# Attention over every 64th key on one core: scores with queries on partitions, the maximum subtracted ahead of exp, weights normalised and turned over by TensorE

## The chip, the cores and the metric

The kernel runs on one core of a Trainium2 chip. The core has five instruction streams that meet only at semaphores: TensorE (PE: matrix products, its weight loads shown as PEld), VectorE (DVE), ScalarE (ACT), GpSimd (POOL) and SyncE (SP, which here only issues DMAs). Sixteen DMA engines carry them out. The metric is the device time of one execution in microseconds (us).

## What is computed

Q, K and V have 8 batches, 12 heads, 1024 rows and 64 columns, in float32. Each of the 1024 queries of a head attends to the 16 keys at rows 0, 64, 128 and so on:

```python
attend_positions = np.arange(0, seq, stride)            # stride 64: 16 keys
scores = np.einsum('bhqd,bhkd->bhqk', q, k) * scale     # scale = 1/8
weights = np.exp(scores - np.max(scores, axis=-1, keepdims=True))
weights = weights / (np.sum(weights, axis=-1, keepdims=True) + 1e-10)
result[:, :, i, :] = np.einsum('bhqk,bhkd->bhqd', weights, v)[:, :, 0, :]
```

Q is read whole (25.17 MB) and the output is written whole (25.17 MB). Of K and V only 1,536 rows of 256 bytes each are read.

## The kernel before

The 96 heads are taken in 24 groups of four (`NG`, `HG`). A group's Q is 1 MB: `load` brings it into one of ten buffers `qn`, 8 KB on each of 128 partitions, and a group's output leaves from one of eight buffers `out_sb` by `store`, 1 MB at a time, or 2 MB for the pairs near the end. In DRAM each partition's piece of an output is written as runs of 4 KB (`send`).

What one group needs, in order:

- `cast`: Q to bfloat16, half by ACT (L328) and half by POOL (L330), into one of two `qb`. POOL's half waits for ACT's, and stands for both.
- `transpose`: DVE turns 32 by 32 blocks of bfloat16 pairs over (L335), so that pairs of the 64 columns lie on partitions, 32 for each of the four heads.
- `score_products`: four products of 512 columns (L469). The stationary operand is `k_t`, the keys of the four heads laid out in blocks with zeros between; Q is the moving one. The result `sc` has **keys on partitions**: 128 partitions are 4 heads by 2 halves of the queries by 16 keys, the free axis holds 512 queries.
- exp by ACT in two instructions of 64 partitions (L353), straight from PSUM, without a maximum, into `w_all`, where zeros stand between.
- `outputs`: eight products of 260 columns (L497), in blocks of 3, 2 and 3 (`blocks`). The stationary operand is a block of `w_all`. The moving one is `v_all`: the values of the group, masked so that each head has its own 64 columns, and four columns of ones, which give the sum of each head's weights. POOL makes it with `values` (L318).
- the division, behind the product: DVE takes reciprocals of the four sums (L453) and multiplies (L459) for blocks 0 and 1. Block 2 is copied by ACT (L383) and multiplied by POOL (L385).

`Program` holds one list of operations, in the order in which the code writes them, with what each reads and writes. `plan` works out the semaphore waits from it, and each engine gets its own operations in that order; nothing is reordered on the chip. PE and DVE run loops written by hand, `pe_stream` with 4 groups in a turn and `dve_stream` with 8. ACT, POOL and SP are unrolled. In the main loop, while group g's output is made, group g+2 is transposed, group g+3 is cast and the scores of g+1 are made.

SP's stream has ten loads first, then `load(g+10)` and `store(g)` in turns, each waiting for what it needs: a load for the buffer to be read out, a store for the output of its group. The very last store is issued behind the loop and waited for at the end.

Of the kernel before, what the change touches and what calls it, by code (L numbers as in the profile page):

```python
# [10 lines left out]
FP32 = mybir.dt.float32  # L11
# [31 lines left out]
class Program:  # L43
# [7 lines left out]
    ENGINES = ("PE", "DVE", "ACT", "POOL", "SP")  # L51

    def __init__(self, nc, tc):
        self.nc, self.tc, self.ops = nc, tc, []
        self.writer, self.readers = {}, {}

    def op(self, engine, fn, reads=(), writes=(), after=(), lane=None, gate=None, gates=(), looped=False, last=False):
# [12 lines left out]
        for k in writes:  # L70
            self.writer[k], self.readers[k] = i, []
        self.ops.append(dict(
            engine=engine, fn=fn, lane=lane or engine, deps=deps, own=own,
            gate=gate, gates=gates, last=last, looped=looped or engine == "PE",
# [3 lines left out]
    def plan(self):  # L78
# [12 lines left out]
        for i, o in enumerate(self.ops):  # L91
            e, waits, gate_waits = o["engine"], [], list(o["gates"])
            for gate, n in o["gates"]:
                assert carriers[gate][n - 1] < i, (i, gate, n)
                learn(e, carriers[gate][n - 1])
            for d in sorted(o["deps"], reverse=True):
# [5 lines left out]
                assert not o["looped"], ("needs more gates", i, e, d, p["lane"])  # L102
# [3 lines left out]
                if d is None:  # L106
                    d = self.ops.index(p)
# [14 lines left out]
        for i, o in enumerate(self.ops):  # L122
            transfer = o["lane"] != o["engine"]
            o["step"] = 16 if transfer else int(i in signals or o["engine"] == "PE" or o["last"])
# [3 lines left out]
            assert o["step"] or o["gate"] or not o["looped"], (i, o)  # L128
# [5 lines left out]
    def emit(self, loops):  # L134
# [7 lines left out]
        gates = {name: nc.alloc_semaphore(f"gate_{name}") for name in names}  # L142
        with self.tc.tile_critical(no_gpsimd_drain=True):  # L143
            for e in ("ACT", "DVE", "POOL"):
                engines[e].addr_align(128, max_nops=0)
            for o in self.ops:
                if o["looped"]:
                    continue
                for gate, n in o["gates"]:
                    engines[o["engine"]].wait_ge(gates[gate], n)  # L150
                for d in o["waits"]:
                    p = self.ops[d]
                    engines[o["engine"]].wait_ge(sems[p["lane"]], p["count"])
                r = o["fn"]()
                if o["gate"]:
                    r.then_inc(gates[o["gate"]], 1)
                elif o["step"]:
                    r.then_inc(sems[o["lane"]], o["step"])
            nc.sync.wait_ge(sems["POOL"], counts["POOL"])
            for loop in loops:  # L160
                loop(sems, gates)
# [5 lines left out]
def kernel(  # L167
# [8 lines left out]
    nc = tc.nc  # L176
# [10 lines left out]
    KW = P + NK  # L187
    TURN = 4
    ROUNDS = 8
    assert B * H == NG * HG and S == 1024 and D == 64 and NK == 16 and NG % TURN == NG % ROUNDS == 0  # L190
    QBUFS = 10
    OBUFS = 8

# [10 lines left out]
    out_all = [sb.tile([P, 2, 4, 8, D], FP32, name=f"out_sb{i}") for i in range(OBUFS // 2)]  # L204
    out_sb = [out_all[i // 2][:, i % 2] for i in range(OBUFS)]
    qt = [sb.tile([P, 32 * D], BF16, name=f"qt{i}") for i in range(2)]
    rec = [sb.tile([P, 8, 4], FP32, name=f"rec{i}") for i in range(2)]
    w_all = sb.tile([P, 2, 8, P], BF16, name="w_all")
    v_all = sb.tile([P, 4, 4 * D + 4], BF16, name="v_all")
    w_bufs, v_bufs = [w_all[:, i] for i in range(2)], [v_all[:, i] for i in range(4)]  # L210
    k_t = sb.tile([P, NG + 1, 2, KW], BF16, name="k_t")
# [3 lines left out]
    perm_v = sb.tile([P, 2, 2, 2, 2, NK], BF16, name="perm_v")  # L215
# [127 lines left out]
    def scores(g):  # L343
# [4 lines left out]
        if g == NG:  # L348
            return
# [197 lines left out]
```

## Time and profile before

| | us |
|---|---|
| median of 3 runs | 127.6 (127.23 to 128.01) |
| the profiled execution's own time | 127.66 |
| its span, from first to last instruction | 125.9 |
| busy: DVE, ACT, POOL, PE | 90.7, 80.9, 78.2, 66.5 |
| DMA packets' share of 16 engines' span | 96.9% |

A row of the groups reads: line, engine, operation, what is written and read with its shape (partitions by elements), how often; then busy time in all and mean ns of one; then the idle time of the engine ahead of it and who ended that. A row of the timeline begins with start and length in us, and an [idle] at its end is what the engine waited ahead of it. In a row of windows stand, behind the stretch and its length, the busy time of PE, PEld, DVE, ACT and POOL, then the granted TensorE clock (1 is full speed), the mean busy share of the DMA engines and their GB/s. The shapes show the free elements of one partition; a matmul's `128x512` has 512 columns.

### The profile page before, as it was taken

The numbers are of one execution on the slowest core, as the hardware profiler recorded it, in microseconds if no ns is written. First come the engines' busy times: TensorE is split into PE (matmuls) and PEld (weight loads), VectorE is DVE, ScalarE is ACT, GpSimd is POOL, SyncE is SP. The second block draws the span as 40 slices with busy tenths as digits, with TensorE's granted clock in tenths as the row PEclk, the third lists the DMA queues.
The fourth block names the chain that finished last, engine by engine and source line by source line (L and its number), as shares of the span: only waits on it lengthen the run. The fifth ranks groups of instructions, "written<-read, shape, count | busy, mean of one in ns | idle before, by whom it ended". The sixth has DMA issues, their size and how long they took to land.

```text
span 125.9 us, 1283 instructions
## 1 busy us (share of the span) xinstructions
PE 66.5 (53%) x296; PEld 29.7 (24%) x296; DVE 90.7 (72%) x161; ACT 80.9 (64%) x103; POOL 78.2 (62%) x89
## 2 busy tenths in 40 slices
PE   0005472887777796466555666478664663840000
PEld 0001130343333333233212333233332320410000
DVE  2996457978669669989997999966999794970000
ACT  4270943686966786989999799968698655711000
POOL 4074247387865956988999699986699851534000
PEclk9999999755685559999999999955999999755555
DMA  1999989899899999899798998999998999999991
GB/s 43 423 312 479 479 354 500 354 479 448 344 417 458 403 435 495 359 474 469 338 515 354 411 515 341 430 458 398 440 482 364 450 427 422 422 422 422 424 424 70
DMA packets 7140, 51.15 MB, mean 406 GB/s; under 512 B 3808, under 2 KB 3808, under 8 KB 3808
## 3 DMA queue, kind: packets, MB, share of 16 engines
q1 hardware_dynamic: 7136, 51.12, 96.9%
q14 instruction: 4, 0.03, 0.1%
HBM read 25.95 MB, written 25.17 MB: 406 GB/s over the span
## 4 chain that ended last, share of the span: by engine, by line
DMA 25%; PE 20%; DVE 20%; ACT 13%; POOL 8%; issue 4%; SPq 1%; ACTq 0%; DVEq 0%; POOLq 0%
DMA out_dram<-out_sb 18%; DVE out_sb L459 12%; PE o L497 10%; PE sc L469 10%; DMA qn<-in_Q_dram 7%; ACT w_all L353 5%; ACT out_sb L383 4%; DVE qt L335 4%; POOL out_sb L385 4%; ACT qb L328 3%; DVE rec L453 3%; POOL qb L330 2%; DVE v_rep L312 1%; POOL v_all L318 1%; SPq L236 1%
## 5 line engine op out<-in xcount | busy, mean ns | idle before, releaser
L497 PE MATMUL o<-v_all,w_all 128*128 128x260 bf16 x192 | 38.8, 327 | 28.5 <-DVE out_sb L459 24.2
L385 POOL TENSOR_TENSOR out_sb<-out_sb,rec 128x768 f32<-128x768 f32 x24 | 35.3, 1472 | 25.3 <-ACT out_sb L383 25.3
L469 PE MATMUL sc<-qt,k_t 128*128 128x512 bf16 x100 | 33.3, 464 | 16.5 <-DVE qt L335 12.3
L459 DVE TENSOR_TENSOR out_sb<-o,rec 128x768 f32<-128x768 f32 (+1 forms) x48 | 39.6, 825 | 1.6
L353 ACT ACTIVATE w_all<-sc 64x512 bf16<-64x512 f32 x48 | 35.2, 733 | 7.3 <-DMA out_dram<-out_sb 3.5
L335 DVE STREAM_TRANSPOSE qt<-qb 128x1024 int32<-128x1024 int32 x26 | 31.6, 1214 | 3.6 <-POOL qb L330 3.5
L497 PEld LDWEIGHTS o<-v_all,w_all 128*128 128x128 bf16 x192 | 18.3, 112 | 52.4 <-DVE out_sb L459 33.0
L383 ACT COPY out_sb<-o 128x768 f32<-128x768 f32 x24 | 19.2, 799 | 16.5 <-DVE rec L453 16.2
L328 ACT CAST qb<-qn 128x1024 bf16<-128x1024 f32 x24 | 25.0, 1045 | 4.3 <-DVE v_rep L312 1.4
L330 POOL CAST qb<-qn 128x1024 bf16<-128x1024 f32 x24 | 24.9, 1039 | 1.9 <-DMA qn<-in_Q_dram 1.7
L453 DVE RECIPROCAL rec<-o 128x12 f32<-128x12 f32 (+1 forms) x72 | 15.4, 213 | 11.7 <-PE o L497 10.9
L318 POOL TENSOR_TENSOR v_all<-mask,v_rep 128x256 bf16<-128x256 bf16 x24 | 16.0, 670 | 4.2 <-DVE v_rep L312 4.1
L469 PEld LDWEIGHTS sc<-qt,k_t 128*128 (+1 forms) x100 | 10.9, 110 | 27.7 <-issue 11.7
L257 DVE MEMSET k_t<- 128x3600 uint32 x1 | 3.1, 3058 | 2.3 <-issue 2.3
L312 DVE CAST v_rep<-o 128x768 bf16<-128x768 f32 x2 | 1.9, 939 | 2.6 <-PE o L302 2.6
L291 DVE COPY k_t<-k_r 32x256 bf16<-32x256 bf16 x8 | 3.2, 395 | 0.1
L277 ACT CAST k_bf<-k_raw 128x256 bf16<-128x256 f32 (+1 forms) x2 | 0.9, 508 | 2.6 <-DMA k_raw<-in_K_dram 2.6
L266 POOL COPY v_all<-s_sel 128x16 bf16<-128x16 bf16 x1 | 0.2, 197 | 3.7 <-DVE s_sel L262 3.7
L277 ACT ACT_TABLE_LOAD x1 | 1.3, 1283 | 1.3 <-SPq L143 1.3
L302 PE MATMUL o<-v_bf,perm_v 128*128 128x384 bf16 x4 | 1.5, 520 | 1.0 <-POOL v_bf L416 1.0
L291 ACT COPY k_t<-k_r 32x128 bf16<-32x128 bf16 x4 | 1.2, 295 | 0.8 <-DVE k_r L279 0.7
L291 POOL COPY k_t<-k_r 32x128 bf16<-32x128 bf16 x4 | 1.2, 290 | 0.3
(13 smaller groups left out, 5.1 us busy)
## 6 DMA issues: line engine op xcount, KB each, us to landing
qn<-in_Q_dram SPq DMA_DIRECT2D x24, 1024.0 KB, 15.4
out_dram<-out_sb SPq DMA_DIRECT2D x16, 1024.0 KB, 14.0
out_dram<-out_sb SPq DMA_DIRECT2D x4, 2048.0 KB, 17.4
k_raw<-in_K_dram SPq DMA_DIRECT2D x1, 384.0 KB, 4.2
v_raw<-in_V_dram SPq DMA_DIRECT2D x1, 384.0 KB, 6.7
```

Source lines behind the costliest of these rows:

```text
L291: op(e, lambda: fn(k_t[dst : dst + 32, 2 * part.start + c : 2 * part.stop : 2, :, col : col + NK], k_r[src : src + 32, part].rearrange("p ...
L318: op("POOL", lambda: nc.gpsimd.tensor_tensor(out=v[:, 0 : 4 * D].rearrange("p (s d) -> p s d", s=4), in0=mask, in1=v_rep[:, g // 2, g % 2] ...
L328: op("ACT", lambda: nc.scalar.copy(b[:, half:], q[:, half:]), reads=[f"qn{g % QBUFS}1"], writes=[f"qb{g % 2}1"])
L330: op("POOL", lambda: nc.gpsimd.tensor_copy(out=b[:, 0:half], in_=q[:, 0:half]), reads=[f"qn{g % QBUFS}0"] + [f"qb{g % 2}1"] * (g >= 2) + [ ...
L335: return nc.vector.transpose(qt[g % 2].bitcast(I32), qb[g % 2].bitcast(I32))
L353: op("ACT", lambda a=a, wa=wa: nc.scalar.activation(out=_ap_with(wa, [wa.ap[0], [P, 8], [1, 2], [2, 32]], extra_offset=64 * a), in_=sc[64 ...
L383: op("ACT", lambda: nc.scalar.copy(to, o), reads=[o_key], writes=[to_key, f"copy{g}"], after=[sums])
L385: op("POOL", lambda: nc.gpsimd.tensor_tensor(out=to, in0=to, in1=by, op=ALU.mult), reads=[to_key, r_key], writes=[to_key], last=g == NG - 1)
L453: sums = dve.reciprocal(r, o_ps[(3 * j + c) % 2][:, 0 : blocks[c][1], 4 * D : 4 * D + 4])
L459: dve.tensor_tensor(out=to, in0=o, in1=by, op=ALU.mult).then_inc(gates["scaled"], 1)
L469: r = pe.matmul(sc_ps[g % 2], lhsT=k_t[:, k, f, NK * (1 - e) : NK * (1 - e) + P], rhs=_ap_with(qt[g % 2], [qt[g % 2].ap[0], [D, 8], [16 * ...
L497: r = pe.matmul(o_ps[(3 * j + c) % 2][:, i, 0 : 4 * D + 4], lhsT=w_bufs[j % 2][:, i0 + i], rhs=v_bufs[j % 4], start=True, stop=True,)
```

## The change

The softmax is moved from the output side to the score side. For each group:

- `cast` also reorders rows, and is split 3/8 ACT (768 elements) and 5/8 POOL (1280). `transpose` writes with a step of four.
- `scores`: Q is now the stationary operand (every second column of `qt`) and the keys the moving one: 16 products of 64 columns, which give 128 queries on partitions and, for 8 tiles of queries by 4 heads, 16 keys along the free axis.
- `lowered`: DVE takes the maximum over each 16 keys (512 elements to 32) and subtracts it (512), from PSUM into `low`, in float32.
- `raised`: one exp of 128 by 512 on ACT, from SBUF.
- `sums`: DVE adds up each 16 (512 elements to 32) and takes 32 reciprocals.
- `weights`: POOL multiplies the 512 weights by their reciprocals into bfloat16.
- `across`: PE turns the weights over with four products against the identity, 128 columns each; `weight_rows`: DVE copies the result (512) from PSUM.
- `outputs`: eight products of 256 columns with 64 rows of weights each; `evict`: ACT copies them out in two instructions of 1024 elements. No division is left there; the columns of ones, the zeros of `w_all` and their memset go.
- `send` writes runs of 2 KB.

In iteration i of the main loop each engine has, in this order:

| engine | operations |
|---|---|
| DVE | `weight_rows(i)`, `transpose(i+3)`, `sums(i+1)`, `lowered(i+2)` |
| PE | `scores(i+2)`, `outputs(i)`, `across(i+1)` |
| ACT | `cast(i+4)`, `evict(i)` twice, `raised(i+2)` |
| POOL | `cast(i+4)`, `values(i+1)`, `weights(i+1)` |

The loops of PE and DVE have two groups in a turn (`PERIOD`), and the last four iterations are unrolled. SP has 15 loads ahead of the first store, then stores and loads in turns.

```diff
-    TURN = 4
-    ROUNDS = 8
+    HK = HG * NK
+    NT = 8
+    PERIOD = 2
+    AHEAD = 4
...
-    o_ps = [ps.tile([P, 3, 512], FP32, name=f"o{i}") for i in range(2)]
+    wt_ps = [ps.tile([P, 512], FP32, name=f"wt_ps{i}") for i in range(2)]
+    o_ps = ps.tile([P, 4, 512], FP32, name="o")
...
+    cut = 5
     def cast(g):
-        q, b = qn[g % QBUFS], qb[g % 2]
-        op("ACT", lambda: nc.scalar.copy(b[:, half:], q[:, half:]),
+        q = qn[g % QBUFS].rearrange("p (j t d) -> p t j d", j=4, t=NT)
+        b = qb[g % 2].rearrange("p (t j d) -> p t j d", t=NT, j=4)
+        op("ACT", lambda: nc.scalar.copy(b[:, cut:], q[:, cut:]),
            reads=[f"qn{g % QBUFS}1"], writes=[f"qb{g % 2}1"])
-        op("POOL", lambda: nc.gpsimd.tensor_copy(out=b[:, 0:half], in_=q[:, 0:half]),
+        did["cast", g] = op("POOL", lambda: nc.gpsimd.tensor_copy(out=b[:, :cut], in_=q[:, :cut]),
            reads=[f"qn{g % QBUFS}0"] + [f"qb{g % 2}1"] * (g >= 2) + ["turn"] * (g < 2),
...
+    def scores(g, i=None):
+            for x in range(NT):
+                t = x // 4 * 4 + x % 2 * 2 + x // 2 % 2
+                for f in range(2):
+                    r = nc.tensor.matmul(
+                        sc_ps[g % 2][:, HK * x : HK * x + HK],
+                        lhsT=q[:, 4 * D * t + f : 4 * D * (t + 1) : 2],
+                        rhs=k_t[:, k, f], start=f == 0, stop=f == 1,
+                    )
...
+    def lowered(g, i=None):
+        maxima = op("DVE", lambda: nc.vector.tensor_reduce(
+            out=top, in_=sc, op=ALU.max, axis=mybir.AxisListType.X,
+        ), reads=[f"sc{g % 2}"], writes=["top"], gates=[did["scored", g]], gate="own", turn=i)
+        op("DVE", lambda: nc.vector.tensor_tensor(
+            out=low[g % 2], in0=sc, in1=top.unsqueeze(2).to_broadcast([P, NT * HG, NK]),
+            op=ALU.subtract,
...
+    def raised(g):
+        did["raised", g] = op("ACT", lambda: nc.scalar.activation(
+            out=ex[g % 2], in_=low[g % 2], func=AF.Exp, bias=0.0, scale=scale,
...
+    def sums(g, i=None):
+        added = op("DVE", lambda: nc.vector.tensor_reduce(
+            out=total, in_=ex[g % 2], op=ALU.add, axis=mybir.AxisListType.X,
+        ), reads=[f"ex{g % 2}"], writes=["total"], gates=[did["raised", g]], gate="own", turn=i)
+        op("DVE", lambda: nc.vector.reciprocal(rec[g % 2], total),
...
+    def weights(g):
+        did["weighed", g] = op("POOL", lambda: nc.gpsimd.tensor_tensor(
+            out=wn[g % 2], in0=ex[g % 2],
+            in1=rec[g % 2].unsqueeze(2).to_broadcast([P, NT * HG, NK]), op=ALU.mult,
...
+    def across(g, i=None):
+            for b in range(NT // 2):
+                r = nc.tensor.matmul(
+                    wt_ps[g % 2][:, P * b : P * b + P], lhsT=w[:, P * b : P * b + P],
+                    rhs=identity, start=True, stop=True,
+                )
...
+    def weight_rows(g, i=None):
+        did["evened", g] = op("DVE", lambda: nc.vector.tensor_copy(
+            out=wt[g % 2], in_=wt_ps[g % 2].rearrange("p (b q) -> p b q", b=NT // 2),
...
+    def outputs(g, i=None):
+                for x in range(4 * n, 4 * n + 4):
+                    b, side = x // 2, x % 2
+                    rows = slice(HK * side, HK * side + HK)
+                    r = nc.tensor.matmul(
+                        o_ps[:, 2 * n + side, HG * D * (b % 2) : HG * D * (b % 2 + 1)],
+                        lhsT=wt[g % 2][rows, b],
+                        rhs=vm[g % 2][rows].rearrange("p h d -> p (h d)"),
...
+            gates = [did["evened", g], did["sent", g - 1]]
...
+    def evict(g):
+        for n in range(2):
+            i = op("ACT", lambda n=n: nc.scalar.copy(
+                out_sb[g % OBUFS][:, :, 4 * n : 4 * n + 4].rearrange("p h t d -> p t h d"),
+                o_ps[:, 2 * n : 2 * n + 2].rearrange("p b (t h d) -> p (b t) h d", t=2, h=HG),
...
     def send(g, n):
-            _ap_with(out, [[16 * D, P], [2 * SD, 2 * n], [1, 16 * D]], g * HG * SD),
+            _ap_with(out, [[NT * D, P], [SD, HG * n], [1, NT * D]], g * HG * SD),
...
+    for i in range(-1, NG):
+        if i >= 0:
+            weight_rows(i, i)
+        if i + 3 < NG:
+            transpose(i + 3, i)
+        if i + AHEAD < NG:
+            cast(i + AHEAD)
+        if i + 1 < NG:
+            sums(i + 1, i)
+        if i + 2 < NG:
+            scores(i + 2, i)
+            lowered(i + 2, i)
+        if i + 1 < NG:
+            values(i + 1)
+            weights(i + 1)
+        g = i - 1
+        if 0 <= g < NG - QBUFS - AHEAD or g == NG - 2:
             store(g, 1)
...
+        if i >= 0:
+            outputs(i, i)
+            evict(i)
+        if i + 2 < NG:
+            raised(i + 2)
+        if i + 1 < NG:
+            across(i + 1, i)
+        for g in range(QBUFS if i < 0 else i + AHEAD + QBUFS, min(i + AHEAD + QBUFS + 1, NG)):
+            load(g)
```

More of the change, by code (lines that the diff above doesn't have):

```diff
@@ L415 @@
     cast(1)
[L416 to L417 removed]
+    did["v_bf"] = op("POOL", lambda: nc.gpsimd.tensor_copy(out=v_bf, in_=v_raw),
+                     reads=["v_raw"], writes=["v_bf"], gate="weighed")
+    lowered(0)
+    raised(0)
+    transpose(1)
     value_rows(0)
[L419 removed]
     value_rows(1)
[L421 to L422 removed]
     cast(2)
[L424 to L439 removed]
+    did["sent", -1] = op("ACT", lambda: nc.scalar.nop(), gate="sent")
```

346 lines of the change are left out of this document (144 added, 202 removed).

## The prediction

> **What bounds the kernel now.** I read the page's header and slices first, then its DMA queues.
>
> ```profile
> span 125.9 us, 1283 instructions
> PE 66.5 (53%) x296; PEld 29.7 (24%) x296; DVE 90.7 (72%) x161; ACT 80.9 (64%) x103; POOL 78.2 (62%) x89
> PEclk9999999755685559999999999955999999755555
> DMA  1999989899899999899798998999998999999991
> GB/s 43 423 312 479 479 354 500 354 479 448 344 417 458 403 435 495 359 474 469 338 515 354 411 515 341 430 458 398 440 482 364 450 427 422 422 422 422 424 424 70
> q1 hardware_dynamic: 7136, 51.12, 96.9%
> ```
>
> No engine is busy for more than 72% of the span; the DMA queue is, for 96.9%, from the second slice to the last but one. The windows give its rate, and the chain of waits, SP's timeline and SP's waits show that the engines wait for it and not it for them:
>
> ```profile
> 30.00:35.00 5.00, 4.05 (x15) 1.84 (x15) 3.79 (x9) 3.25 (x5) 3.57 (x5) 0.64 1.05 444
> 60.00:70.00 10.00, 5.42 (x32) 2.69 (x32) 9.14 (x17) 9.14 (x12) 9.15 (x10) 1.00 1.00 423
> 80.00:90.00 10.00, 7.45 (x29) 3.55 (x30) 7.49 (x15) 7.19 (x10) 7.15 (x8) 0.66 1.00 423
> 120.00:126.00 6.00, 0.00 (x0) 0.00 (x0) 0.00 (x0) 0.00 (x0) 0.00 (x0) 0.50 0.55 232
> 82.78 22.47 DMA out_dram<-out_sb
> 25.45 0.63 SPq L34 DMA_DIRECT2D out_dram<-out_sb  x1
> 58.49 0.59 SPq L34 DMA_DIRECT2D out_dram<-out_sb  x1
> 61.86 0.59 SPq L34 DMA_DIRECT2D out_dram<-out_sb  x1
> 108.40 7.89 SPq L34 DMA_DIRECT2D out_dram<-out_sb  x3
> SPq L542 <- DMA out_dram<-out_sb: 8.7, 1, 8.7
> ```
>
> Two megabytes (a load and a store) at 423 GB/s are 2.10/0.423 = 4.96 us, so the queue needs 4.96 us for each of 24 groups. Between the stores at 58.49 and 61.86 the engines need 3.37 us: they run ahead, until ACT waits 22.47 us for an old store to leave its buffer. Still the last store's issue ends at 108.40 + 7.89 = 116.29, and SP then waits 8.7 us. So the engines' chain has only some 10 us to spare: once its groups take so long that the last output comes later than that, it ends the kernel, and the question is the time per group, c.
>
> **The change part by part.** Prices, from groups by shape and from the timeline (starts of neighbours):
>
> ```profile
> L385 POOL TENSOR_TENSOR out_sb<-out_sb,rec 128x768 f32<-128x768 f32 x24 | 35.3, 1472 | 25.3 <-ACT out_sb L383 25.3
> L318 POOL TENSOR_TENSOR v_all<-mask,v_rep 128x256 bf16<-128x256 bf16 x24 | 16.0, 670 | 4.2 <-DVE v_rep L312 4.1 <-POOL out_sb L385 0.2
> L330 POOL CAST qb<-qn 128x1024 bf16<-128x1024 f32 x24 | 24.9, 1039 | 1.9 <-DMA qn<-in_Q_dram 1.7
> L416 POOL CAST v_bf<-v_raw 128x768 bf16<-128x768 f32 x1 | 0.8, 819 | 0.0
> L328 ACT CAST qb<-qn 128x1024 bf16<-128x1024 f32 x24 | 25.0, 1045 | 4.3 <-DVE v_rep L312 1.4 <-DMA qn<-in_Q_dram 0.8
> L277 ACT CAST k_bf<-k_raw 128x512 bf16<-128x512 f32 x1 | 0.6, 612 | 0.0
> L353 ACT ACTIVATE w_all<-sc 64x512 bf16<-64x512 f32 x48 | 35.2, 733 | 7.3 <-DMA out_dram<-out_sb 3.5 <-PE sc L469 3.3
> L383 ACT COPY out_sb<-o 128x768 f32<-128x768 f32 x24 | 19.2, 799 | 16.5 <-DVE rec L453 16.2
> L453 DVE RECIPROCAL rec<-o 128x12 f32<-128x12 f32 x48 | 10.6, 221 | 11.7 <-PE o L497 10.9
> L453 DVE RECIPROCAL rec<-o 128x8 f32<-128x8 f32 x24 | 4.7, 198 | 0.0
> L262 DVE TENSOR_REDUCE s_sel<-identity 128x4 bf16<-128x128 bf16 x1 | 0.2, 228 | 0.0
> L312 DVE CAST v_rep<-o 128x768 bf16<-128x768 f32 x2 | 1.9, 939 | 2.6 <-PE o L302 2.6
> ```
>
> ```profile
> 9.21 1.25 DVE L335 STREAM_TRANSPOSE qt<-qb 128x1024 int32<-128x1024 int32 x1
> 61.98 0.69 DVE L459 TENSOR_TENSOR out_sb<-o,rec 128x512 f32<-128x512 f32 x1
> 62.59 0.22 DVE L453 RECIPROCAL rec<-o 128x12 f32<-128x12 f32 x1
> 62.84 1.25 DVE L335 STREAM_TRANSPOSE qt<-qb 128x1024 int32<-128x1024 int32 x1
> 64.01 0.20 DVE L453 RECIPROCAL rec<-o 128x12 f32<-128x12 f32 x1
> ```
>
> DVE: a 512-element pass over PSUM lasts 0.69, and the next, if it needn't wait for the result, starts 0.61 behind it (62.59 - 61.98); the transpose takes 1.17 (64.01 - 62.84), and its step of four is left unpriced, since no row has one. A reduction over 512 has no row: 0.23 for 128 elements from below, 0.69 (one pass of this length) from above; I take 0.69, the same length. The reciprocal of 32: the step from 8 to 12 elements adds 23 ns, so 20 more add 0.12 to 0.22, 0.34; at least 0.2; I take 0.3. A group is then weight_rows 0.61, transpose 1.17, sum 0.69, reciprocal 0.3, maximum 0.69, subtraction 0.69: **4.15**. Removed are three reciprocals and two multiplications.
>
> ACT: cast of 768 between 612 and 1045, 0.83; eviction of 1024 by the slope of the casts, (1045 - 612)/512 = 0.85 ns each, 0.80 + 256 x 0.00085 = 1.01, twice; exp 0.73 as in its row (128 partitions cost a cast no more than its elements): **3.58**. POOL: cast of 1280 by its slope (1039 - 819)/256, 1.26; values 0.67; weights of 512 between 1472 x 2/3 = 0.98 and the line through 670 and 1472, 1.07; I take 1.03: **2.96**. PE needs rows of its own, at full and at half clock:
>
> ```profile
> 58.35 0.23 PEld L497 LDWEIGHTS o<-v_all,w_all 128*128 128x128 bf16 x3 [1.22 <-DVE out_sb L459]
> 58.35 0.51 PE L497 MATMUL o<-v_all,w_all 128*128 128x260 bf16 x3 [0.94 <-DVE out_sb L459]
> 25.55 0.35 PEld L497 LDWEIGHTS o<-v_all,w_all 128*128 128x128 bf16 x3 [1.37 <-DVE out_sb L459]
> 25.56 0.83 PE L497 MATMUL o<-v_all,w_all 128*128 128x260 bf16 x3 [0.89 <-DVE out_sb L459]
> 52.44 1.07 PE L469 MATMUL sc<-qt,k_t 128*128 128x512 bf16 x4 [0.84 <-issue]
> core 0: 125.9 us, clock 0.823
> ```
>
> A weight load paces at 0.077 (full) or 0.117 (half), a product of 260 columns at some 0.113 or 0.217 with 0.17 of filling. With 64 columns behind each load the 16 score products go at the loads' pace, 1.23 or 1.87; at worst load and product stand one behind the other (64/260 of a product more), 1.68 or 2.72. I take the pace, since loads ran under products in every row. Four output products take 0.45 or 0.87, across 4 loads and the filling, 0.48 or 0.65. The turn of PE's loop costs 0.84 with nothing waited for, now every second group.
>
> Each engine alone is thus below 4.96. What sets c is **that they wait for each other in a circle**. POOL's cast(i+4) stands ahead of its weights(i+1) and waits for ACT's cast(i+4), which stands behind raised(i+1), which waits for DVE's lowered(i+1). Followed by durations:
>
> - Circle A, two groups long: exp 0.73, ACT cast 0.83, POOL cast 1.26, values 0.67, weights 1.03, across 0.48, four handovers of 0.04 (estimate; see the neighbours above), then DVE's 4.15: 9.30, or 4.65 a group.
> - Circle B goes through PE and the evictions, which stand ahead of raised on ACT: loop turn 0.84, scores 1.23, four outputs 0.45 and 0.17, two evictions 2.02, exp 0.73, casts 0.83 + 1.26, values 0.67, weights 1.03, across 0.48, handovers 0.1: 9.8, or **4.90** a group. At half clock 0.64 + 0.42 + 0.17 more, 11.04 or **5.52**; with loads and products apart 5.12 and 5.95.
>
> The granted clock was 0.823, that is half clock for 35% of the span (1 - 0.823 = 0.5 x 0.354). With the same share, c = 4.90 + 0.354 x 0.62 = **5.12**.
>
> [...]
>
> Head: in place of the first store at 25.45. DVE turns group 0 over by 10.46 as now (its casts are longer by 0.2, the memset ahead of it shorter); then scores at half clock 1.87, maximum and subtraction 1.38, transpose, two copies of values (0.94 each), transpose, sum and reciprocal 5.2, weights 1.03, across 0.65, weight_rows and four outputs 1.66, evictions 2.02: 24.3, and with handovers and a wait for a cast **25**.
>
> End: 23 more groups, 117.8; the last four have no cast in their circle, -(0.83 + 1.26)/2 each, -4.2. Then issue 0.6, 1.05 MB at 423 GB/s 2.5, and from the end of the data (120 + 0.55 x 6 = 123.3) to the span's end 2.6: 5.7. Span 25 + 117.8 - 4.2 + 5.7 = 144.3 against 125.9; the profiled run took 127.66, 1.8 more than its span, and the median is 127.6: **146.1**.
>
> Costed at nothing: the halved runs of the stores and the 15 loads ahead of the first store (15.7 MB, 37 us of queue; each load still lands long before its group). Their cover is the queue itself, which has 24 x (5.12 - 4.96) and more to spare; without it they are the next case's price.
>
> **The rivals.**
>
> 1. *The queue still ends last*, so not slower. The place is SP's last store: if the circles are loose (if a cast runs while its engine would wait), it is issued by 116.29. The point is 25 + 23c - 4.2 = 116.3, c = 4.15, which is just DVE's own sum. Time 127.6; at the best window's 444 GB/s, 51.12 MB take 5.7 us less, 122. For it speaks that DVE alone would allow it; against, that both circles go in written order. Runs of 2 KB could take something off:
>
> ```profile
> k_raw<-in_K_dram SPq DMA_DIRECT2D x1, 384.0 KB, 4.2
> ```
>
>    K's 96 pieces of 256 bytes per engine take 4.2 - 2.6 = 1.6 us where 423 GB/s give 0.93: 7 ns a piece; 384 more pieces per engine are at most 2.7 us, 130.3. Against it: stores of 4 KB runs and the loads before them both move about 422.
> 2. *Full clock throughout, or a loop turn that hides*: c = 4.65 to 4.90, 135.3 to 141.
> 3. *Half clock throughout*: 5.52 to 5.95, 155.3 to 165. [...]
>
> **How the numbers follow.** Mixed clock, c 4.95 to 5.4, 142 to 152: 0.45. Rival 2: 0.23. Rival 3: 0.22. Rival 1: 0.08, half of it faster. Something unnamed and slower still: 0.02. The predicted time is 146. The range 132 to 160 leaves out the queue's case, the worst half clock and what is unnamed. A measurement of this kernel can tell about 0.5% from no change: faster 0.04, same 0.04, slower 0.92.
>
> **What would show it.** In the changed profile the DMA digits fall to 8 or 7 behind the first third and GB/s to some 2.1/5.1 = 410 or less; stores are issued about 5.1 us apart to the end; SP's wait at the end is near 5 us; POOL's weights follow values with little gap in one of two groups, DVE's weight_rows waits for across, and raised follows the second eviction at once. Wrong it would be if DMA stays at 9 to the end (rival 1), if stores keep 3.4 to 4.2 us apart, if one pass on DVE or POOL lasts far beyond its price (the reductions, the transpose with its step), or if the head is later than 25 by more than 3 us.

## The result and the profile after

The changed kernel takes 153.84 us (median of 4, 153.70 to 154.04), the kernel before 127.65 beside it: a ratio of 1.205, interval 1.202 to 1.209. So it is 20% slower. The page's header, slices and queue of the changed kernel, beside those of before in the prediction:

```profile
span 152.1 us, 2049 instructions
PE 62.7 (41%) x676; PEld 41.7 (27%) x676; DVE 121.0 (80%) x158; ACT 82.3 (54%) x103; POOL 74.1 (49%) x86
DMA  3999999999998999999999998076094093941995
GB/s 83 349 472 414 422 457 431 457 435 414 414 412 377 427 448 448 407 390 431 470 416 381 431 392 366 4 276 276 0 353 198 30 396 125 384 168 69 396 407 231
q1 hardware_dynamic: 6848, 51.12, 82.0%
```

The bytes are the same; the packets' share fell from 96.9 to 82.0%. The queue is full for the first 25 slices, as long as there are loads to do ahead, and then has holes: it waits for the engines. SP's timeline (start, length) and its wait at the end say how far apart the outputs come:

```profile
29.61 0.63 SPq L34 DMA_DIRECT2D out_dram<-out_sb  x1
34.95 0.59 SPq L34 DMA_DIRECT2D out_dram<-out_sb  x1
...
77.68 69.36 SPq L34 DMA_DIRECT2D out_dram<-out_sb  x9
SPq L579 <- DMA out_dram<-out_sb: 4.2, 1, 4.2
```

Stores are 5.34 us apart from the first one on, where the queue alone would need 4.96, and the last issue ends at 77.68 + 69.36 = 147.04 in place of 116.29. The span is made of 29.6 for the first store, 23 x 5.34 = 122.8, less 6.0 at the last groups (the difference), and 5.7 behind the last issue's start. The windows carry the granted clock in the last column but two:

```profile
60.00:70.00 10.00, 5.11 (x56) 3.45 (x56) 8.76 (x12) 6.21 (x8) 5.19 (x7) 1.00 1.00 420
```

It is 1.00 in every window read, 0.823 on the mean before. The groups by shape and the chain of waits of the changed kernel:

```profile
DVE 59%; POOL 18%; PE 10%; DMA 4%; issue 3%; ACT 1%; SPq 0%; POOLq 0%
L465 ACT COPY out_sb<-o 128x1024 f32<-128x1024 f32 x48 | 46.2, 1015 | 24.7 <-PE o L450 24.7
L372 DVE STREAM_TRANSPOSE qt<-qb 128x1024 int32<-128x1024 int32 x24 | 48.7, 2027 | 1.2 <-POOL qb L365 1.2
L365 POOL CAST qb<-qn 128x1280 bf16<-128x1280 f32 x24 | 30.0, 1250 | 38.5 <-ACT qb L363 35.6
L420 POOL TENSOR_TENSOR wn<-ex,rec 128x512 bf16<-128x512 f32 x24 | 25.4, 1057 | 24.7 <-DVE rec L416 24.7
L440 DVE CAST wt<-wt_ps 128x512 bf16<-128x512 f32 x24 | 16.6, 692 | 14.9 <-PE wt_ps L429 14.9
```

Two things stand out. The transpose lasts 2.03 us in place of 1.25. And POOL's weights wait for DVE's reciprocal in all 24 groups, while DVE's weight_rows wait for PE, which has turned those weights over. The timeline of one group shows that these two waits are one circle:

```profile
71.50 0.69 DVE L440 CAST wt<-wt_ps 128x512 bf16<-128x512 f32 x1 [0.57 <-PE wt_ps L429]
72.11 2.04 DVE L372 STREAM_TRANSPOSE qt<-qb 128x1024 int32<-128x1024 int32 x1
73.99 0.62 DVE L413 TENSOR_REDUCE total<-ex 128x32 f32<-128x512 f32 x1
74.65 0.35 DVE L416 RECIPROCAL rec<-total 128x32 f32<-128x32 f32 x1
75.08 1.06 POOL L420 TENSOR_TENSOR wn<-ex,rec 128x512 bf16<-128x512 f32 x1 [0.82 <-DVE rec L416]
76.19 0.61 PE L429 MATMUL wt_ps<-identity,wn 128*128 128x128 bf16 x4 [2.91 <-POOL wn L420]
76.84 0.69 DVE L440 CAST wt<-wt_ps 128x512 bf16<-128x512 f32 x1 [0.56 <-PE wt_ps L429]
```

From start to start: weight_rows(i) 0.61, transpose(i+3) 1.88, sums(i+1) 0.66, reciprocal 0.43, weights(i+1) 1.11, across(i+1) 0.65, and weight_rows(i+1) begins. The sum is 5.34 us, the whole distance between groups. Call it circle C. It spans one group, and the transpose of a group two further on lies in it only because DVE's list has it between weight_rows and sums.

### The profile page after: what moved, and what is told of

The parts are those of the page before. It is cut to its first block, busy times and chain, and to the rows that moved or that the text cites. A ratio compares the mean times of both kernels' runs of the same rounds, so it can differ in the third digit from the quotient of the medians.

```text
span 152.1 us, 2049 instructions
## 1 busy us (share of the span) xinstructions
PE 62.7 (41%) x676; PEld 41.7 (27%) x676; DVE 121.0 (80%) x158; ACT 82.3 (54%) x103; POOL 74.1 (49%) x86
## 3 DMA queue, kind: packets, MB, share of 16 engines
q1 hardware_dynamic: 6848, 51.12, 82.0%
## 4 chain that ended last, share of the span: by engine, by line
DVE 59%; POOL 18%; PE 10%; DMA 4%; issue 3%; ACT 1%; SPq 0%; POOLq 0%
DVE qt L372 31%; POOL wn L420 17%; DVE wt L440 11%; PE wt_ps L429 10%; DVE total L413 8%; DVE rec L416 6%; DMA qn<-in_Q_dram 4%; DVE k_t L326 2%; ACT out_sb L465 1%; DVE v_rep L347 1%; POOL qb L365 1%; DVE top L399 0%; PE o L450 0%; SPq L278 0%; DVE low L402 0%
## 5 line engine op out<-in xcount | busy, mean ns | idle before, releaser
L465 ACT COPY out_sb<-o 128x1024 f32<-128x1024 f32 x48 | 46.2, 1015 | 24.7 <-PE o L450 24.7
L372 DVE STREAM_TRANSPOSE qt<-qb 128x1024 int32<-128x1024 int32 x24 | 48.7, 2027 | 1.2 <-POOL qb L365 1.2
L365 POOL CAST qb<-qn 128x1280 bf16<-128x1280 f32 x24 | 30.0, 1250 | 38.5 <-ACT qb L363 35.6
L420 POOL TENSOR_TENSOR wn<-ex,rec 128x512 bf16<-128x512 f32 x24 | 25.4, 1057 | 24.7 <-DVE rec L416 24.7
L386 PE MATMUL sc<-k_t,qt 128*128 (+1 forms) x384 | 25.8, 242 | 18.8 <-DVE qt L372 13.2
L408 ACT ACTIVATE ex<-low 128x512 f32<-128x512 f32 x24 | 15.1, 630 | 30.2 <-DVE low L402 30.1
L386 PEld LDWEIGHTS sc<-k_t,qt 128*128 128x128 bf16 x384 | 23.0, 131 | 22.3 <-DVE qt L372 13.9
L440 DVE CAST wt<-wt_ps 128x512 bf16<-128x512 f32 x24 | 16.6, 692 | 14.9 <-PE wt_ps L429 14.9
L450 PE MATMUL o<-vm,wt 64*128 64x256 bf16 x192 | 24.8, 410 | 1.6 <-DVE wt L440 1.6
L363 ACT CAST qb<-qn 128x768 bf16<-128x768 f32 x24 | 19.6, 817 | 4.7 <-DMA qn<-in_Q_dram 3.3
L402 DVE TENSOR_TENSOR low<-sc,top 128x512 f32<-128x512 f32 x24 | 16.6, 691 | 0.8
```

The source lines that it names most:

```text
L363: op("ACT", lambda: nc.scalar.copy(b[:, cut:], q[:, cut:]), reads=[f"qn{g % QBUFS}1"], writes=[f"qb{g % 2}1"])
L365: did["cast", g] = op("POOL", lambda: nc.gpsimd.tensor_copy(out=b[:, :cut], in_=q[:, :cut]), reads=[f"qn{g % QBUFS}0"] + [f"qb{g % 2}1"] * ...
L372: "DVE", lambda: nc.vector.transpose(qt[g % 2].bitcast(I32).rearrange("p (t q j) -> p t j q", t=NT, j=4), qb[g % 2].bitcast(I32).rearrange ...
L386: r = nc.tensor.matmul(sc_ps[g % 2][:, HK * x : HK * x + HK], lhsT=q[:, 4 * D * t + f : 4 * D * (t + 1) : 2], rhs=k_t[:, k, f], start=f == ...
L402: op("DVE", lambda: nc.vector.tensor_tensor(out=low[g % 2], in0=sc, in1=top.unsqueeze(2).to_broadcast([P, NT * HG, NK]), op=ALU.subtract,) ...
L420: did["weighed", g] = op("POOL", lambda: nc.gpsimd.tensor_tensor(out=wn[g % 2], in0=ex[g % 2], in1=rec[g % 2].unsqueeze(2).to_broadcast([P ...
```

## The experiments

The theory at this point: circle C sets the pace; its two faults are the transpose's step of four (0.7 us) and the transpose's place ahead of the sums. Rivals: DVE has too much to do (its busy share of 80%), or circle A of the prediction, through casts, would hold the pace anyway.

**The step taken out.** DVE transposes flat, and weight_rows puts the queries in order with a stepped read from PSUM.

```diff
-                qt[g % 2].bitcast(I32).rearrange("p (t q j) -> p t j q", t=NT, j=4),
-                qb[g % 2].bitcast(I32).rearrange("p (t j q) -> p t j q", t=NT, j=4),
+                qt[g % 2].bitcast(I32), qb[g % 2].bitcast(I32),
...
-            out=wt[g % 2], in_=wt_ps[g % 2].rearrange("p (b q) -> p b q", b=NT // 2),
+            out=wt[g % 2].rearrange("p b (q j) -> p b q j", j=4),
+            in_=wt_ps[g % 2].rearrange("p (b j q) -> p b q j", b=NT // 2, j=4),
```

> The transpose on DVE writes without a step, and the copy of the turned-over weights (weight_rows) puts the queries in order instead, reading PSUM with a step of 32. Theory (the circle weight_rows, transpose, sums, weights, across, one group long, sets 5.34 us a group, and 0.83 of it is the step of the transpose): the transpose goes from 2.03 to 1.2, groups follow each other by 4.5 to 4.6, the time falls by some 18 us to 134 to 138. Rival 1 (the two-group circles through the casts and the evictions bind at once behind it, at 4.65 to 4.90): 138 to 144. Rival 2 (the transpose takes 2.03 for its shape or for GpSimd beside it, not for the step): stays at 2.03 and 153.8. If the stepped read of PSUM costs what it saves, weight_rows goes from 0.69 to 1.5 and the time stays above 150.

Measured 136.56 us, ratio 1.067 (1.064 to 1.071). The timeline of one group:

```profile
71.92 0.69 DVE L439 CAST wt<-wt_ps 128x512 bf16<-128x512 f32 x1 [0.56 <-PE wt_ps L428]
72.53 1.24 DVE L372 STREAM_TRANSPOSE qt<-qb 128x1024 int32<-128x1024 int32 x1
73.69 0.64 DVE L412 TENSOR_REDUCE total<-ex 128x32 f32<-128x512 f32 x1
74.02 0.67 POOL L352 TENSOR_TENSOR vm<-mask,v_rep 128x256 bf16<-128x256 bf16 x1
74.37 0.35 DVE L415 RECIPROCAL rec<-total 128x32 f32<-128x32 f32 x1
74.80 1.06 POOL L419 TENSOR_TENSOR wn<-ex,rec 128x512 bf16<-128x512 f32 x1
75.91 0.61 PE L428 MATMUL wt_ps<-identity,wn 128*128 128x128 bf16 x4 [2.21 <-POOL wn L419]
76.56 0.69 DVE L439 CAST wt<-wt_ps 128x512 bf16<-128x512 f32 x1 [0.57 <-PE wt_ps L428]
```

Groups are 4.64 us apart and weight_rows still takes 0.69: the stepped read from PSUM costs nothing here. So two thirds of the loss, 17 of 26 us, are that step.

The pace is still that of circle C, which has become shorter by the step: 0.61, 1.16, 0.68, 0.43, 1.11 and 0.65 from start to start, 4.64 in all. The weights start 0.43 behind the reciprocal, as in the changed kernel, and 0.78 behind values, where 0.63 is enough if nothing holds them (see the version with both edits below). The list of POOL's waits has this one in only 4 groups; the gap on POOL is 0.11 us (74.02 + 0.67 = 74.69 to 74.80), easily overlooked. How far circle A lies below, that version shows too.

**Maximum and subtraction left out**, exp straight from PSUM:

```diff
-            out=ex[g % 2], in_=low[g % 2], func=AF.Exp, bias=0.0, scale=scale,
+            out=ex[g % 2], in_=sc_ps[g % 2].rearrange("p (x k) -> p x k", k=NK),
+            func=AF.Exp, bias=0.0, scale=scale,
...
-            lowered(i + 2, i)
```

> The maximum and its subtraction are left out (exp straight from PSUM), so DVE has 1.3 us less to do for each group. Theory (circle of one group): the two passes lie in the wait for the turned-over weights, outside the circle, so groups still follow each other by 5.3, DVE's wait ahead of weight_rows grows from 0.6 to 1.9, and the time falls only by the head's two passes, to 150 to 153. Rival (DVE's own work, busy for 80% of the span, is the bound): 5.34 - 1.3 = 4.0 to 4.1 a group and 127 to 131.

Measured 152.13 us, ratio 1.189 (1.183 to 1.194). DVE's timeline:

```profile
75.20 0.69 DVE L441 CAST wt<-wt_ps 128x512 bf16<-128x512 f32 x1 [1.84 <-PE wt_ps L430]
80.54 0.69 DVE L441 CAST wt<-wt_ps 128x512 bf16<-128x512 f32 x1 [1.84 <-PE wt_ps L430]
```

DVE has 1.27 us a group less to do and waits 1.27 longer (1.84 for 0.57), and the groups stay 5.34 apart. The subtraction of the maximum, which gives the change half its name, costs nothing in the steady state; the 1.7 us saved lie in the first and last groups. DVE's busy share is not the bound.

**Sums ahead of the transpose** on DVE, step kept:

```diff
+        if i + 1 < NG:
+            sums(i + 1, i)
         if i + 3 < NG:
             transpose(i + 3, i)
...
-        if i + 1 < NG:
-            sums(i + 1, i)
```

> On DVE the sums and reciprocals of group i+1 stand ahead of the transpose of group i+3, nothing else. Theory: the transpose leaves the circle of one group, which shrinks to 3.4; what binds next is the circle of two groups through exp, both casts, values, weights and across back to DVE's own 4.77: (5.1 + 4.8)/2 = 4.95 a group, 143 to 147. Rival (DVE's own work alone): 4.77 and 140 to 142. Rival (order doesn't matter): 153.8.

Measured 143.67 us, ratio 1.122 (1.117 to 1.128), groups 4.9 us apart. Circle C without the transpose is 5.34 - 1.88 = 3.46 and no longer binds. What fits the new pace is circle A, which holds one transpose in two groups: by the prediction's terms, with the step added, (9.30 + 0.72)/2 = 5.0, and by the 9.12 that it takes without the step in the version with both edits below, (9.12 + 0.72)/2 = 4.92.

**Which side of the step costs.** First the step on the reading side of the transpose alone:

```diff
-                qt[g % 2].bitcast(I32).rearrange("p (t q j) -> p t j q", t=NT, j=4),
-                qb[g % 2].bitcast(I32).rearrange("p (t j q) -> p t j q", t=NT, j=4),
+                qt[g % 2].bitcast(I32).rearrange("p (t j q) -> p t j q", t=NT, j=4),
+                qb[g % 2].bitcast(I32).rearrange("p (t q j) -> p t j q", t=NT, j=4),
```

> The transpose reads and writes with the same step of four, where the changed kernel only writes with it, so the queries come out in another order. If a step on the reading side costs as much again as one on the writing side, it goes from 2.03 to 2.8 and the time to 170; if only the writing side costs, it stays at 2.03 and 153.8.

> The transpose reads with a step of four and writes without one, so the queries come out in another order. If a step on either side costs the same, it stays at 2.03 and the time at 153.8; if only writing with a step costs, it falls to 1.2 to 1.25 and the time to 136 to 138.

Both of these were run with this one edit, and nothing else: the first has the step on the reading side alone too, whatever its expectation says of the writing side. So they are one kernel executed twice, 155.82 and 155.93 us. The transpose's row (of the first; 2029 ns in the second):

```profile
L372 DVE STREAM_TRANSPOSE qt<-qb 128x1024 int32<-128x1024 int32 x24 | 48.7, 2028 | 1.2 <-POOL qb L365 1.2
```

Then the step on both sides:

```diff
-                qb[g % 2].bitcast(I32).rearrange("p (t j q) -> p t j q", t=NT, j=4),
+                qb[g % 2].bitcast(I32).rearrange("p (t q j) -> p t j q", t=NT, j=4),
```

> The changed kernel with the step of four on the reading and on the writing side of the transpose (the queries come out in another order). In the two kernels e4_readstep and e7_readonly, which turned out to be one and the same edit, the step stood on the reading side alone and the transpose took 2.03 us, as with the step on the writing side alone. Theory (the two sides do not add up, since one pass waits for the slower side): the transpose takes 2.0 to 2.1 us, groups 5.3 to 5.5 us apart, 153 to 156. Rival (the sides add up): 1.24 + 2 x 0.79 = 2.8 us, groups 6.1 apart, about 170.

One execution, 156.37 us:

```profile
L372 DVE STREAM_TRANSPOSE qt<-qb 128x1024 int32<-128x1024 int32 x24 | 49.7, 2073 | 1.3 <-POOL qb L365 1.3
```

By the length of the transpose, written or read, the step costs the same 0.79 us; on both sides, 0.83. The two hardly add up. What counts for the pace is how soon the next pass starts: 1.16 behind a flat transpose, 1.88 behind one that writes with the step, and 1.96 behind one that reads with it or does both (from DVE's timelines). So groups are 5.44 us apart in these three executions in place of 5.34, which is why they take some 2 us longer than the changed kernel; the last one is just above the range expected.

**The step alone in the kernel before:**

```diff
-        return nc.vector.transpose(qt[g % 2].bitcast(I32), qb[g % 2].bitcast(I32))
+        return nc.vector.transpose(
+            qt[g % 2].bitcast(I32).rearrange("p (t q j) -> p t j q", t=8, j=4),
+            qb[g % 2].bitcast(I32).rearrange("p (t j q) -> p t j q", t=8, j=4),
+        )
```

> The kernel before, with nothing changed but the step of four on the writing side of its transpose, so the queries come out in another order. Theory: 0.83 us more on DVE in each group makes its 3.37 at full clock 4.2, still below the queue's 4.96, so the price that costs the changed kernel 17 us costs here nothing: 127 to 129. Rival (the step is a loss wherever it stands): 24 x 0.83 = 20 more, 148.

A miss: 131.0 to 133.4 us in four executions; the ratio of the two shorter ones is 1.032 (1.024 to 1.039). From the profile of the longest, SP's first and last stores and the chain of waits by engine:

```profile
27.57 0.63 SPq L34 DMA_DIRECT2D out_dram<-out_sb  x1
83.48 43.69 SPq L34 DMA_DIRECT2D out_dram<-out_sb  x7
DVE 51%; PE 31%; issue 8%; POOL 3%; ACT 3%; DVEq 0%; SPq 0%
```

No DMA is left in that chain: the engines end this kernel. Its stores come 4.30 us apart, (83.48 - 27.57)/13, where those of the kernel before come 3.89 apart, (76.04 - 25.45)/13, and the last issue ends at 127.17 for 116.29. The transpose lasts 1.99 for 1.21, which makes 19 us in 24 groups. DVE itself takes up 7 of them: its wait for PE ahead of the reciprocals falls from 10.9 to 4.0 us. Most of the rest, 10.9 us, arrives at the last issue. Behind it SP waited 8.7 us in the kernel before and waits 3.6 here, so 5 more are covered by the queue, and the end comes 3.5 to 6 us later. The four times go with the granted clock (0.81 and 0.83 in the two of 133.4, 0.86 and 0.89 in the others), which fits engines that end last.

The cover is there, but finite. The expectation compared one period at full clock, 4.2, with the queue's 4.96. What has to hold is the time of the last store: with the first at 25.45, a group may take (116.3 - 25.45)/23 = 3.95 us until the last issue moves at all.

**Flat, and sums first:**

Both of the edits shown above together.

> Both repairs at once: the transpose without a step and, on DVE, sums and reciprocals ahead of the transpose. Theory: the circle of one group is now 3.4 and DVE's own work 3.95, but the circle of two groups (exp, ACT's cast, POOL's cast, values, weights, across: 5.1; then DVE's 3.95) still gives 4.5 a group, so this is hardly better than the flat transpose alone: 133 to 136. Rival (DVE's own work is what is left): 3.95 to 4.0 a group, and the DMA queue ends last, 127 to 129.

134.32 us, ratio 1.053 (1.048 to 1.058). The timeline, over two groups:

```profile
70.59 0.69 DVE L439 CAST wt<-wt_ps 128x512 bf16<-128x512 f32 x1
73.14 0.67 POOL L352 TENSOR_TENSOR vm<-mask,v_rep 128x256 bf16<-128x256 bf16 x1
73.77 1.06 POOL L419 TENSOR_TENSOR wn<-ex,rec 128x512 bf16<-128x512 f32 x1
79.71 0.69 DVE L439 CAST wt<-wt_ps 128x512 bf16<-128x512 f32 x1
```

The weights now follow values at once, 0.63 behind, so the reciprocal no longer holds them. Circle A is what is left, through POOL's list, where the cast stands ahead of the weights: from exp at 70.52 through both casts, values, weights, across and DVE's list to exp at 79.64 are 9.12 us, for two groups. That is 4.56 a group, only 0.08 below the 4.64 of the flat version, so that taking the transpose out of C gains little here. Circle B, which passes no DVE, can't be longer than 9.12 either.

**Weights first on POOL**, values a group earlier in four buffers, the loops of PE and DVE with four groups in a turn, on top of the two edits above:

```diff
-        if i + AHEAD < NG:
-            cast(i + AHEAD)
...
             weights(i + 1)
+        if i + AHEAD < NG:
+            cast(i + AHEAD)
+        if i + 2 < NG:
+            values(i + 2)
```

> As the run with both repairs, and on POOL weights(i+1) stand ahead of cast(i+4), with values made one group earlier in four buffers; the loops of PE and DVE take four groups in a turn, so that the buffers are known in it. Theory: the circle through the casts is cut, DVE's 3.95 to 4.0 a group is left, below the 4.15 at which the DMA queue ends last: 126.5 to 129, no difference from the kernel before that can be told, with the maximum subtracted. Rival 1 (the circle through the evictions is longer than I add up): 4.3 or more a group and above 131. Rival 2 (runs of 2 KB slow the queue once it is the bound): 129 to 131.

129.08 us, ratio 1.012 (1.008 to 1.015), just above the range expected; groups 4.17 apart, DVE waiting for exp for 0.10 to 0.17 of that. What the longer turn alone gives was not tried.

**The transpose first on DVE, casts one group further ahead:**

```diff
-    AHEAD = 4
+    AHEAD = 5
...
+        if i + 3 < NG:
+            transpose(i + 3, i)
         if i >= 0:
             weight_rows(i, i)
...
-        if i + 3 < NG:
-            transpose(i + 3, i)
```

> As the version with flat transpose, sums early and weights first on POOL, with two things moved: DVE turns group i+3 over ahead of weight_rows(i) and sums(i+1), and the casts run one group further ahead (five), so that the transpose waits for a cast of the turn before. In that version the groups followed each other by 4.17 us, of which DVE waited 0.10 to 0.17 for exp, with only weight_rows (0.66) between the subtraction and the sums that need exp (0.63 and two handovers). Theory (DVE's own sum is what is left, and below some 4.05 us a group the DMA queue ends last again): exp now lies behind transpose and weight_rows (1.77 us) and costs nothing; period 4.0 to 4.05, last store issued near 116, DMA share 97%, time 127.3 to 128.3, no difference from before that can be told. Rival (another wait takes its place, or the runs of 2 KB slow the queue): period stays at 4.17 or the queue moves less than 420 GB/s where only stores are left, 128.5 to 130.

A miss, of the rival's kind and above its range too: 131.51 us, ratio 1.029 (1.025 to 1.032), groups 4.33 apart. The timeline:

```profile
59.25 1.24 DVE L372 STREAM_TRANSPOSE qt<-qb 128x1024 int32<-128x1024 int32 x1
...
62.04 0.35 DVE L415 RECIPROCAL rec<-total 128x32 f32<-128x32 f32 x1
62.43 0.83 ACT L363 CAST qb<-qn 128x768 bf16<-128x768 f32 x1 [1.14 <-DVE rec L415]
63.16 1.92 ACT L465 COPY out_sb<-o 128x1024 f32<-128x1024 f32 x2
64.97 0.64 ACT L407 ACTIVATE ex<-low 128x512 f32<-128x512 f32 x1
65.65 0.69 DVE L412 TENSOR_REDUCE total<-ex 128x32 f32<-128x512 f32 x1 [0.25 <-ACT ex L407]
66.37 0.35 DVE L415 RECIPROCAL rec<-total 128x32 f32<-128x32 f32 x1
```

ACT's cast needs the transpose, which had ended at 60.49, but starts behind the reciprocal. `plan` lets an operation with a `gate` signal only the engine that the gate is for; ACT is given the next one without a gate, and transpose, weight_rows and the sum's reduction all have one. So reciprocal, cast, two evictions, exp and sums follow each other: 4.33.

**The same, with the transpose signalling ACT:**

```diff
-            writes=[f"qt{g % 2}"], gate="turned", gates=[did["cast", g]], turn=i)
+            writes=[f"qt{g % 2}"], gate="turned" if g < 2 else None, gates=[did["cast", g]], turn=i)
...
-            writes=[f"sc{g % 2}"], gates=[did["turned", g]], gate="scored", turn=i)
+            writes=[f"sc{g % 2}"], gates=[did["turned", g]] if g < 2 else [], gate="scored", turn=i)
```

> As the version before (flat transpose first on DVE, casts five groups ahead), but the transpose signals ACT itself. In the version before ACT's cast waited 1.14 us a group for DVE's reciprocal, because the transpose, weight_rows and the sums carry signals for PE and DVE alone and the reciprocal was the next instruction behind them that ACT could wait for; its groups followed each other by 4.33 us. Now PE learns of the transpose through the signals it waits for anyway, and ACT's cast starts behind the transpose. Theory (that wait took the place of the one removed): ACT's idle time ahead of its cast goes, the circle reciprocal, ACT cast, two evictions, exp, sums no longer binds, period 4.0 to 4.05 (DVE's own sum), last store issued near 116, and the DMA queue ends last: 127.3 to 128.5. Rival (runs of 2 KB slow the queue, or there is a further circle): period above 4.1 or stores alone below 415 GB/s, 128.5 to 131.

129.18 us, ratio 1.012 (1.009 to 1.014). DVE's timeline, the queue, and a window late in the kernel where only stores are left:

```profile
61.35 1.23 DVE L372 STREAM_TRANSPOSE qt<-qb 128x1024 int32<-128x1024 int32 x1
65.33 1.24 DVE L372 STREAM_TRANSPOSE qt<-qb 128x1024 int32<-128x1024 int32 x1
q1 hardware_dynamic: 6848, 51.12, 96.5%
110.00:115.00 5.00, 2.35 (x21) 1.15 (x20) 2.33 (x4) 2.62 (x4) 1.23 (x2) 1.00 1.00 416
```

The pace is 3.98 us, below the 4.96 of the queue, and the queue is full to the end: the wait is gone as the theory had it. The time is above its range and in the rival's, and 1.2% remain.

**The shorter stores alone,** the kernel before with the changed kernel's store pattern:

```diff
-            _ap_with(out, [[16 * D, P], [2 * SD, 2 * n], [1, 16 * D]], g * HG * SD),
+            _ap_with(out, [[8 * D, P], [SD, HG * n], [1, 8 * D]], g * HG * SD),
```

> The kernel before with one line changed: its stores write runs of 2 KB at the addresses of the changed kernel in place of runs of 4 KB (the output's rows come out in another order). Compute is as before, whose engines have some 10 us to spare, so only the queue can show a difference. Theory (the 1.2% by which the two fastest versions still trail the kernel before, at full DMA digits, are the shorter runs): 128.8 to 129.5, and 415 to 418 GB/s in the stretch 110 to 115 where only stores are left, for 423 before. Rival (the runs cost nothing, and what is left comes from the later first store or from the engines): 127.2 to 128.0 and 423 GB/s.

Between the two: 128.47 us, ratio 1.004 (1.001 to 1.007), a third of the 1.2%. The same window in this kernel:

```profile
110.00:115.00 5.00, 2.62 (x12) 1.06 (x10) 3.19 (x6) 1.58 (x2) 1.47 (x1) 0.84 1.00 419
```

The other 1 us or so of the last version, where the queue moves about 416 GB/s, is open; the order of loads and stores differs, and that wasn't tried. No version is faster than the kernel before: all of them move the same 51.12 MB, and the queue was busy for 96.9% of the span there already.

## Why the prediction came out as it did

The sign and the mechanism held: the engines, which wait for each other in a circle, need more than the queue's 4.96 us a group, and the queue no longer ends last. 153.84 lies in the range, 7.8 above the forecast: the head is 4.6 longer and 23 groups 5.0 (5.34 for 5.12), the last groups gain 1.8 more. But the circle that sets the pace is not the one that the forecast rests on, and that 5.12 came so near is luck. The step of the transpose and the circle that it lies in were left out; against that, circle B was too long and half clock never came.

1. *"Its step of four is left unpriced, since no row has one."* This is the step that failed. No bound was put on it from above, and the trace of before shows none, since its transposes (L279 and L335) are all flat. It costs 1.88 - 1.16 = 0.72 us a group, start to start (2.03 for 1.24 in length, 2.07 with the step on both sides), and the flat version is 17 us faster. The run of the kernel before with this step alone gives nearly the same price, 1.99 for 1.21.
2. *The list of circles.* A and B were followed through casts and evictions, both two groups long; C wasn't listed. At the prediction's own prices it is 0.61 + 1.17 + 0.69 + 0.3 + 1.03 + 0.48 and three handovers of 0.04, 4.40: it would not have ruled. Measured, it is 4.64 flat, with across (0.65 for 0.52 with its handover), the reciprocal and its handover to POOL (0.43 for 0.34) and the weights and theirs (1.11 for 1.07), and 5.34 with the step. Flat, it is already ahead of A and B, by 0.08; the step, which lies in C in every group and in A in every second, widens that. That C binds is shown twice: taking the step out of it shortened the pace by C's own 0.70, and moving the transpose out of it freed the pace, which came to 4.9, where A is.
3. *Circles A and B.* A is borne out: 9.30 for two groups, and 9.12 measured in the flat version with sums first. B, the one that gave the forecast's 4.90 at full clock, is not: it takes 9.12 at most in place of 9.8. Scores (1.06 for 1.23), the wait at the turn of PE's loop (0.58 for 0.84) and exp (0.63 for 0.73) were shorter than priced, and passes that start before the one ahead has ended were added whole (two evictions of 1.015 us take 1.93). In the changed kernel it does not bind either, as ACT's exp waits for DVE's subtraction in 23 groups (30.1 us in all), and not for the second eviction.
4. *The clock.* "With the same share" half of full speed added 0.22 a group. The clock was full throughout (1.00 in all four executions), so by this step alone c was too high, and by the prediction's terms full clock gives the 135 to 141 of rival 2; the version where C does not bind and the step is out takes 134.3. Full clock with C and the step gives 153.8. The lengths bear the clock out: eight output products of 256 columns take 1.03 us, 0.13 each, where 260 columns took 0.113 at full clock (1.00 from 58 to 62) and 0.217 at half clock (0.50 from 25 to 30) before. PE's busy time does not order the clock in these traces: here PE is busy 41% with waits of 2.9 us in it and is granted 1.00, while 53% of before got 0.823; and within before the window 80 to 90 had PE busy for 7.45 us of 10 at 0.66, the window 60 to 70 for 5.42 at 1.00. No run shows the half clock throughout of rival 3: every version of the changed kernel was granted 1.00. What sets the clock here stays open.
5. *DVE's sum of 4.15*: 5.34 - 0.57 = 4.77 measured, 0.72 of it the step; without the step 4.07 in the flat version, and 3.98 in the version that DVE and the queue alone bound. The reductions were sized well (0.63 for 0.69), as were the eviction (1.015 for 1.01), POOL's cast (1.25 for 1.26), the weights (1.06 for 1.03) and the cast on ACT (0.82 for 0.83); exp was 0.63 on 128 partitions for 0.73, the row of 64. Sixteen score products took 1.06 for 1.23.
6. *Head*: 25 forecast, 29.6 measured, beyond the 3 us named. Two parts of it show in the changed kernel's timeline:

```profile
24.82 1.93 ACT L465 COPY out_sb<-o 128x1024 f32<-128x1024 f32 x2 [0.58 <-PE o L450]
28.77 0.81 ACT L363 CAST qb<-qn 128x768 bf16<-128x768 f32 x1
```

   The first group's evictions end at 26.75, 1.8 later than forecast. But the store is issued 2.9 later still, at 29.61, right behind ACT's next cast (28.77 + 0.81 = 29.58): the second eviction and exp carry signals with a `gate`, so that SP, like ACT in the experiment with the transpose first, waits for the next operation without one. The forecast let the store follow the eviction. Of the 1.8, the step in three transposes is worth 2.2, and another item was left out of the list of the head, four copies of keys on DVE ahead of the first maximum; parts of the head that were shorter than forecast gave some back:

```profile
11.10 2.73 DVE L326 COPY k_t<-k_r 32x256 bf16<-32x256 bf16 x4
11.13 1.04 PE L386 MATMUL sc<-k_t,qt 128*128 128x64 bf16 x16 [11.13 <-DVE qt L372]
```

   The scores are ready at 12.17 and DVE is free at 13.84, 1.7 later; the scores' own full clock gave back 0.8. The flat version has its first store at 26.42, so 3.2 of the 4.6 go with the step, directly and through the circle. *End*: 5.7 as forecast. The last groups gain 6.0 for 4.2, and not for the reason given: with no transpose left the last two come 3.5 us apart in place of 5.34 (3.7 together), and the last stores no longer wait for a cast.
7. *Rival 1* fell for the kernel as changed, but its point, c = 4.15, was well placed: with 4.17 and 3.98 a group the queue stays full and the time is within 1.2% of before, with 4.33 it is 3% above. The "10 us to spare" were too many, though: the kernel before waits 8.7 us behind its last issue where the changed one needs 4.2, so 4.5 us are free, and a later issue moves the end. Its runs of 2 KB, priced at 2.7 us at most, cost 0.5 (0.1 to 0.9). *Rival 3* fell with the clock.

Of what was to show it, the waits of DVE for across and of SP at the end (4.2 for about 5) were right. The DMA digits fell, but only behind 25 of 40 slices, and to 0 in places. `raised` does not follow the second eviction at once, since it waits for the subtraction. POOL's weights follow values *with* a gap in every group (0.82 of waiting for the reciprocal), which is the mark of circle C. And "one pass on DVE lasts far beyond its price (... the transpose with its step)" had been named as a way to be wrong, and it was the one.

## What to carry to other kernels

Before adding up an engine's instructions, list every circle of waits, the shortest included, and look for work in it that belongs to another group and stands there only by the order of the list: the transpose cost 10 us there (153.8 to 143.7) by its place alone. A changed access pattern is a changed instruction (2.03 us for 1.24 here): price it, and where no row shows one, by a run of the kernel before with that pattern alone (1.99 for 1.21 there). Close the sum of start times to see which circle binds: in the flat version the wait that told it was 0.11 us long. And where an engine has room to spare, say how much, and by when: 7 us of it on DVE and 5 behind the last store did not hide 19.

## What the runs showed of the hardware

- A STREAM_TRANSPOSE of 128 by 1024 words took 1.24 us in the flat version (1.19 to 1.24 in all flat ones), 2.03 with a step of four words on the writing side in the changed kernel (1.97 to 2.03 in all with it) or on the reading side, and 2.07 with both; the next pass on DVE started 1.16, 1.88 (writing), 1.96 (reading) and 1.96 us (both) behind it.
- A copy of 512 elements from PSUM with a step of 32 elements on its reading side took 0.69 us in the flat version (0.66 to 0.69 in all with it), and 0.69 without it in the changed kernel.
- The TensorE clock was 1.00 throughout in all versions of the changed kernel, with PE busy 41 to 49%, and 0.82 to 0.86 in the profiled executions of the kernel before with and without edits, with PE busy 52 to 55%.
- Sixteen pairs of a weight load and a product of 64 columns took 1.06 us, 66 ns a pair, in the changed kernel at a granted clock of 1.00.
